# Differential attention: the 32 rotary rows of a head's query and key tiles gathered by DMA, turned together, and put back

## The chip, the cores and the metric

The kernel runs on one core of one Trainium2 chip. The metric is the time of one launch in microseconds (us) of the device, as the median of several runs. TensorE is called PE here, VectorE DVE, ScalarE ACT, GpSimd POOL and SyncE SP, as the profile does.

## The reference, cut to what matters

Two transformer blocks of two layers each on 512 tokens of width 1024, in float32. The second mixer of the first block is differential attention with 8 heads. Each head has two query and two key parts of 64 dimensions, and the first 16 dimensions of every part are rotated:

```python
def _rope(x, positions, theta):          # x: (..., d), d = 16 here
    ang = positions * theta ** (-arange(0, d, 2) / d)
    x1, x2 = x[..., :d // 2], x[..., d // 2:]
    return concatenate([x1 * cos(ang) - x2 * sin(ang), x2 * cos(ang) + x1 * sin(ang)], -1)

q, k, v = split(x @ w_qkv, 3)            # q, k: 16 parts of 64, rope on the first 16 of each
p1, p2 = causal_softmax(q1 @ k1.T / 8), causal_softmax(q2 @ k2.T / 8)
o = (p1 - lam * p2) @ v                  # per head, 128 wide
o = rmsnorm(o, subln) * (1 - lambda_init)
return o.reshape(b, s, 1024) @ w_o
```

## The kernel before

The program is a row of eight phases: latent attention, a feed-forward layer, differential attention (`diff`), a feed-forward layer, then the four layers of the second block. All activations stay on chip; weights stream in by DMA on SP's queue into two buffers (`raw`). Each fp32 matmul is done as three products of a high and a low part (lines 347 to 349: high by high, low by high, high by low). For that every weight tile is cast into `whi` by ACT (line 313) and its rest `wlo` is formed by DVE (line 314), up to five tiles ahead.

In `diff`, q and k of a head are 128x512 tiles (rows: two parts of 64 dimensions; columns: tokens), made in PSUM by 24 matmuls each (`pj`; `ps` for the first two heads). `evac(h, which)` takes a finished tile: `rope` turns it, then `split` and a copy cast it into what the score matmuls read: two casts `qa` and four casts `ka` on ACT (64x512 each), the low part of q on POOL, the low part of k on DVE (`xd`). These lines of `rope` are what the change replaces, 16 tiles in all:

```python
nc.vector.stream_shuffle(t2, src, swap)                   # L653, 128x512, from PSUM
nc.vector.tensor_tensor(t1, src, C, op=ALU.mult)          # L654
nc.vector.tensor_tensor(t2, t2, Sn, op=ALU.mult)          # L655
nc.gpsimd.tensor_tensor(t1, t1, t2, op=ALU.add)           # L656
```

`scores(h, qt)` makes the two score tiles `s` of a block of 128 queries (128 x 128, 256, 384 and 512 columns for qt 0 to 3), DVE takes the row maxima (L589), ACT the exponentials (L592), DVE joins both (`xc`, L1041 to L1043), PE transposes the result (`pt`, L353), ACT and DVE split it (`xa`, `xb`), and `value` multiplies it by V (`o`). `post` takes the norm: ACT squares and copies `o` (L1050, L1052), PE sums (`sps`), POOL takes the power (`rr`, L1067), PE spreads it (`bp`), DVE multiplies (L1074), ACT and POOL split the result into `VH` and `VL`.

Between the score groups the projection of the next head is spread (`fills`, table `n`), and work that follows a result is put off by `defer(delay, f)`: it is issued once the matmuls written since have passed the delay on a clock that counts matmul columns. A scheduler then orders PE, ACT, DVE and SP by its own estimates; POOL keeps the order of the program in `diff`. The first 128x128 scores of head h+1 follow the 128x512 scores of head h.

Of the kernel before, what the change touches and what calls it, by code (L numbers as in the profile page):

```python
# [9 lines left out]
F32 = mybir.dt.float32  # L10
F32R = mybir.dt.float32r
I32 = mybir.dt.int32
AF = mybir.ActivationFunctionType
ALU = mybir.AluOpType
# [3 lines left out]
D = 1024  # L18
S = 512
# [3 lines left out]
LAMBDA_INIT = 0.8 - 0.6 * math.exp(-0.3)  # L23
DFF1, DFF2 = 4096, 2816
MLA_SWAP = [i ^ 16 for i in range(32)]
DIFF_SWAP = [i ^ 8 if i < 16 else i for i in range(32)]
RING = 5
RAW = 2
AUTO = True
# [1 line left out]

PLAN = {
    "mla": dict(hand=("SP", "Pool"), ln=7000, sm=6000, pv=2500, eb=3, gate=5, cq=1500, n=([5] * 4 + [6] * 4) * 3 + [5] * 4 + [9] * 4),
    "diff": dict(hand=("Pool",), qp=1, kp=0, vp=1, wp=0, rp=0, nb=2, ln=7000, rot=3500, sm=6500, pv=2500, eb=3, sums=1000, scale=5500, n=[30] * 4 + [11] * 24 + [9] * 4),
    "fox": dict(ln=5500, sm=4200, pv=1500, eb=2, n=[30] * 4 + [11] * 24 + [9] * 4),
    "ret": dict(ln=5500, y=3900, n=30),
    "f0": dict(ln=7000), "f1": dict(ln=8500), "g0": dict(ln=5500), "g1": dict(ln=5500),
# [3 lines left out]
class Net:  # L41
# [617 lines left out]

    def rope_tables(self, pool, tmp, which, tags=("t0", "t1", "t2"), bufs=1):  # L660
        nc = self.nc
        C = pool.tile([128, S], F32, name="ropeC", bufs=1)
        Sn = pool.tile([128, S], F32, name="ropeS", bufs=1)
        pi = tmp.tile([128, S], I32, tag=tags[0], name="pi", bufs=bufs)
        a = tmp.tile([128, S], F32, tag=tags[1], name="ang", bufs=bufs)
        k = tmp.tile([128, S], F32, tag=tags[2], name="kk", bufs=bufs)
        inv = self.col[:, 2 * which:2 * which + 1]
        sgn = self.col[:, 2 * which + 1:2 * which + 2]
        (nc.gpsimd if which else nc.sync).dma_start(out=pi, in_=self.A["positions"].to_broadcast([128, S]))
        nc.vector.tensor_copy(a, pi)  # L670
        nc.vector.tensor_scalar(a, a, inv, None, op0=ALU.mult)
        MAG = 12582912.0
        nc.vector.tensor_scalar(k, a, 1.0 / (2 * math.pi), MAG, op0=ALU.mult, op1=ALU.add)
        nc.vector.tensor_scalar(k, k, -MAG, None, op0=ALU.add)
        c1 = 6.28125
        c2 = float(np.float32(2 * math.pi - c1).view(np.int32) & -4096)
        c2 = float(np.int32(np.float32(2 * math.pi - c1).view(np.int32) & -4096).view(np.float32))
        c3 = float(np.float32(2 * math.pi - c1 - c2))
        for cc in (c1, c2, c3):
            nc.vector.scalar_tensor_tensor(a, k, -cc, a, op0=ALU.mult, op1=ALU.add)  # L680
        PIF = 3.1415925
        nc.vector.tensor_scalar(a, a, PIF, -PIF, op0=ALU.min, op1=ALU.max)
        nc.scalar.activation(Sn, a, AF.Sin)
        nc.vector.scalar_tensor_tensor(a, a, -1.0, a, op0=ALU.mult, op1=ALU.min)
        nc.vector.tensor_scalar(a, a, math.pi / 2, None, op0=ALU.add)
        nc.scalar.activation(C, a, AF.Sin)
        nc.vector.tensor_scalar(Sn, Sn, sgn, None, op0=ALU.mult)
        return C, Sn

    def setup(self):  # L690
# [268 lines left out]
    def diff(self):  # L959
        nc, A, tc = self.nc, self.A, self.tc  # L960
        mm = nc.tensor.matmul
        with ExitStack() as outer:
# [27 lines left out]
            kls = [kz[:, 2 * i:2 * i + 2, :] for i in range(2)]  # L990
            places = self.whole("c", F32)

            def evac(h, which):
                def f(ps):
                    r = self.rope(p, ps, DIFF_SWAP, C, Sn)


                    if which == 0:
                        qk[h] = [self.rs(n, F32R).rearrange("p (a n) -> p a n", a=2) for n in ("qa", "ka")]
                        qk[h].append(kls[h % 2])  # L1000
                    q, k, kl = qk[h]
                    for i in range(2):
                        own, other = slice(64 * i, 64 * i + 64), slice(64 - 64 * i, 128 - 64 * i)
                        if which == 0:
                            self.split(q[own, i, :], q[other, i, :], r[own], eng=nc.gpsimd if self.plan["qp"] else None)
                        else:
                            self.split(k[own, i, :], kl[own, i, :], r[own], eng=nc.gpsimd if self.plan["kp"] else None)
                            nc.scalar.copy(k[other, i, :], r[own])
                    ready.add((h, which))
                return f  # L1010

            self.fhead(4, lambda i, ps: evac(i // 2, i % 2)(ps))
            for _ in self.v_half(VH, VL, 0):
                pass

# [32 lines left out]
            def post(h, o):  # L1048
                sq = places[:, 3, :]
                nc.scalar.activation(sq, o, AF.Square)  # L1050
                ot = p.tile([128, S], F32, tag="ot", name="ot", bufs=1)
                nc.scalar.copy(ot, o)  # L1052
                rr = self.small(4, "rr")

                def sums():
                    sps = self.ps("sps")
                    for t in range(NT):
                        mm(sps[:, 2 * t:2 * t + 2], sq[:, t * 128:t * 128 + 128], ones, start=(t == 0), stop=(t == NT - 1))
                        self.tick(128, 4)
                    s8 = self.small(8, "s8")  # L1060
                    nc.vector.tensor_copy(s8, sps[:, 0:8])

                    nc.vector.tensor_tensor(rr, s1[h], s1[h], op=ALU.mult)
                    nc.vector.tensor_scalar(rr, rr, 1e-6, None, op0=ALU.mult)
                    nc.vector.scalar_tensor_tensor(rr, s8.rearrange("p (t a) -> p t a", a=2)[:, :, 0], 1.0 / 128, rr,
                                                   op0=ALU.mult, op1=ALU.add)
                    nc.gpsimd.tensor_tensor(rr, rr, self.mh, op=ALU.pow)  # L1067
                    self.defer(self.plan["scale"], scale)

                def scale():  # L1070
                    bp = self.ps("bp")
                    for t in range(NT):
                        self.transpose(bp[:, t * 128:t * 128 + 128], rr[:, t:t + 1].to_broadcast([128, 128]))
                    nc.vector.scalar_tensor_tensor(ot, ot, sub, bp, op0=ALU.mult, op1=ALU.mult)  # L1074
                    self.split(VH[:, h, :], VL[:, h, :], ot, eng=nc.gpsimd if self.plan["vp"] else None)
                    nready[0] = h + 1

                self.defer(self.plan["sums"], sums)
# [334 lines left out]
ROPE_ORDER = np.array([16 * (i // 32) + i % 16 + 32 * (i % 32 // 16) for i in range(64)])  # L1413


def constants():
    c = {}
    c["c_idn"] = np.eye(128, dtype=np.float32)
    i = np.arange(128)
    c["c_mask"] = np.zeros((128, S), np.float32)  # L1420
    c["c_mask"][:, S - 128:] = np.where(i[None, :] <= i[:, None], 0.0, NEG)
    col = np.zeros((128, 16), np.float32)
    col[:, 0] = (10000.0 ** (-2.0 * (ROPE_ORDER[i % 64] % 32) / 64.0)).astype(np.float32)
    col[:, 1] = np.where(ROPE_ORDER[i % 64] < 32, -1.0, 1.0)
    d = i % 64
    col[:, 2] = np.where(d < 16, 500000.0 ** (-2.0 * (d % 8) / 16.0), 0.0).astype(np.float32)
    col[:, 3] = np.where(d < 8, -1.0, np.where(d < 16, 1.0, 0.0))
    c["c_col"] = col
    rows = np.zeros((32, 16), np.float32)
    r = np.arange(32)  # L1430
    kind = r // 8
    rows[:, 0] = kind == 0
    rows[:, 1] = kind == 1
    rows[:, 2] = kind >= 2
    rows[:, 3] = -1.0 * (kind == 2)
    rows[:, 4] = -1.0 * (kind == 3)
    rows[:, 5] = kind < 2
    rows[r, 8 + r % 8] = 1.0
    c["c_rows"] = rows
    inv = (10000.0 ** (-np.arange(128) / 128.0)).astype(np.float32)  # L1440
    ang = (np.arange(S, dtype=np.float32)[None, :] * inv[:, None]).astype(np.float32).astype(np.float64)
    c["c_rcos"] = np.cos(ang).astype(np.float32)
    c["c_rsin"] = np.sin(ang).astype(np.float32)
    key, q = np.arange(128)[:, None], np.arange(S)[None, :]
    dec = np.zeros((4, 128, S), np.float32)
    for h in range(4):
        gam = 1.0 - 2.0 ** (-5.0 - h)
        dec[h] = np.where(q // 64 >= key // 64, gam ** np.abs(q - key), 0.0)
    c["c_decay"] = dec
    return c  # L1450


def layout(I):
    A = dict(constants())
# [36 lines left out]
        A[f"w_in{i}"] = gu.reshape(n // 2, 4, 128, D)[1:]  # L1491
        A[f"w_out{i}"] = pack_h(np.asarray(I["ffn_w_out_2"])[i])

    def heads(w):
        q, k = pack_f(w[:, :D]), pack_f(w[:, D:2 * D])
        v = np.concatenate([pack_v(np.ascontiguousarray(w[:, 2 * D + j * 512:2 * D + j * 512 + 512])) for j in range(2)])
        qk = np.stack([q, k], axis=1).reshape(16, 128, D)
        return np.concatenate([qk[:4], v, qk[4:]])

    A["w_d"] = heads(np.asarray(I["diff_w_qkv"])[0])  # L1500
    A["w_do"] = pack_h(np.asarray(I["diff_w_o"])[0])
    wx = np.asarray(I["fox_w_in_2"])[0]
    A["w_x"] = heads(wx[:, :3 * D])
# [29 lines left out]
```

## Time and profile before

| | us |
|---|---|
| median of 3 runs | 2502.1 (2501.55 to 2502.84) |
| profiled execution, its own time | 2498.99 |
| span in the profile | 2497.1 |
| PE busy | 2443.6 (98%) |
| DVE busy | 1655.0 (66%) |
| ACT busy | 1114.1 (45%) |
| POOL busy | 347.9 (14%) |

The span runs from the first to the last instruction; the execution's own time holds 1.9 us more around it. Busy time is time in which an instruction runs on the engine. PE is busy nearly throughout, so the end of the kernel moves by what PE's idle stretches gain or lose. `diff` lies at about 545 to 800 us of the span.

### The profile page before, as it was taken

What the parts mean: (1) busy time and instruction counts of PE and PEld (TensorE: products, weight loads), DVE (VectorE), ACT (ScalarE), POOL (GpSimd) and SP (SyncE); (2) the same over time, 40 slices, a digit from 0 to 9 for tenths busy, and PEclk for the clock granted to TensorE, in tenths of its full rate; (3) what the DMA queues carried; (4) which work ended last, traced back from release to release, by engine and by line L of the source; (5) the groups of instructions that cost most, each with busy time, mean ns of one, the idle gap of its engine ahead of it and who ended that gap; (6) DMA issues with size and microseconds to landing.
All of it is one profiled execution on the core that took longest, in us unless ns stands there. A gap on an engine that the chain in (4) does not pass through costs nothing.

```text
span 2497.1 us, 35898 instructions
## 1 busy us (share of the span) xinstructions
PE 2443.6 (98%) x14612; PEld 2173.6 (87%) x14612; DVE 1655.0 (66%) x2294; ACT 1114.1 (45%) x1664; POOL 347.9 (14%) x311
## 2 busy tenths in 40 slices
PE   8999999999989999999999999999999999999998
PEld 7889889887778988987888999988888888999987
DVE  6978758656987956755655877744455455777743
ACT  5634535424663543544454544543322233444532
POOL 2103012012342201103000222100000000222100
PEclk9999999999999999999999999999999999999999
DMA  4323232323121333232312233232422223233232
GB/s 151 109 68 116 92 107 88 102 79 93 60 85 51 119 99 106 83 110 77 94 59 85 90 114 102 85 102 77 129 82 82 87 85 101 85 121 108 77 102 76
DMA packets 65861, 233.41 MB, mean 93 GB/s; under 512 B 7536, under 2 KB 7680, under 8 KB 65696
## 3 DMA queue, kind: packets, MB, share of 16 engines
q1 hardware_dynamic: 62064, 219.21, 27.4%
q0 software_dynamic: 3488, 11.55, 1.5%
q8 instruction: 114, 1.87, 0.3%
q14 instruction: 51, 0.42, 0.1%
q10 hardware_dynamic: 144, 0.36, 0.0%
HBM read 228.99 MB, written 2.10 MB: 93 GB/s over the span
## 4 chain that ended last, share of the span: by engine, by line
PE 52%; DVE 1%; issue 0%; ACT 0%; POOL 0%; DMA 0%; DVEq 0%; POOLq 0%; ACTq 0%
PE zA L266 3%; PE zA L267 3%; PE zA L268 3%; PE ta L348 2%; PE ta L349 2%; PE ta L347 2%; PE tb L348 2%; PE tb L347 2%; PE tb L349 2%; PE ps L347 2%; PE ps L348 2%; PE ps L349 2%; PE pj L347 2%; PE pj L349 2%; PE pj L348 2%; PE v L347 2%
## 5 line engine op out<-in xcount | busy, mean ns | idle before, releaser
L314 DVE TENSOR_TENSOR wlo<-raw,whi 128x1024 fp32r<-128x1024 f32 (+3 forms) x347 | 432.8, 1249 | 294.2 <-ACT whi L313 293.8
L313 ACT CAST whi<-raw 128x1024 fp32r<-128x1024 f32 (+3 forms) x347 | 359.5, 1038 | 579.4 <-PE ta L349 129.1
L314 DVE TENSOR_TENSOR wlo<-qt,whi 128x1024 fp32r<-128x1024 f32 x102 | 164.2, 1610 | 36.8 <-ACT whi L313 36.8
L347 PE MATMUL ps<-XH,whi 128*128 128x256 f32 (+1 forms) x576 | 178.6, 310 | 2.3 <-ACT XH L313 2.3
L348 PE MATMUL ps<-XL,whi 128*128 128x256 f32 (+1 forms) x576 | 177.5, 308 | 0.1
L349 PE MATMUL ps<-XH,wlo 128*128 128x256 f32 (+1 forms) x576 | 177.1, 308 | 0.0
L267 PE MATMUL zB<-XL,whi 128*128 128x256 f32 x544 | 154.0, 283 | 0.4 <-DVE XL L314 0.4
L266 PE MATMUL zB<-XH,whi 128*128 128x256 f32 x544 | 154.0, 283 | 0.0
L268 PE MATMUL zB<-XH,wlo 128*128 128x256 f32 x544 | 153.9, 283 | 0.0
L313 ACT CAST whi<-qt 128x1024 fp32r<-128x1024 f32 x102 | 107.1, 1050 | 91.8 <-PE zA L267 59.6
L196 POOL TENSOR_TENSOR qt<-qr,raw 128x1024 f32<-128x1024 f32 x34 | 87.1, 2560 | 367.6 <-PE ta L348 204.2
L349 PE MATMUL ta<-whi,jt 128*128 128x512 f32 x320 | 124.1, 390 | 3.0 <-DVE jt L314 3.0
L196 POOL TENSOR_TENSOR qt<-raw,qt 128x1024 f32<-128x1024 f32 x34 | 87.7, 2579 | 272.6 <-DVE wlo L314 248.1
L347 PE MATMUL ta<-whi,jt 128*128 128x512 f32 x320 | 124.8, 390 | 0.0
L348 PE MATMUL ta<-wlo,jt 128*128 128x512 f32 x320 | 124.6, 389 | 0.0
L347 PEld LDWEIGHTS ps<-XH,whi 128*128 128x128 f32 x576 | 110.5, 192 | 7.5 <-ACT XH L313 2.6
L347 PE MATMUL pj<-XH,whi 128*128 128x512 f32 x288 | 116.7, 405 | 0.0
L348 PEld LDWEIGHTS ps<-XL,whi 128*128 128x128 f32 x576 | 110.6, 192 | 5.7 <-DVE XL L314 0.8
L349 PEld LDWEIGHTS ps<-XH,wlo 128*128 128x128 f32 x576 | 110.5, 192 | 5.1
L349 PE MATMUL pj<-XH,wlo 128*128 128x512 f32 x288 | 113.0, 392 | 0.0
L348 PE MATMUL pj<-XL,whi 128*128 128x512 f32 x288 | 112.5, 391 | 0.0
L267 PEld LDWEIGHTS zB<-XL,whi 128*128 128x128 f32 x544 | 104.4, 192 | 0.6 <-DVE XL L314 0.6
(469 smaller groups left out, 7378.7 us busy)
## 6 DMA issues: line engine op xcount, KB each, us to landing
raw<-in_w_r SPq DMA_DIRECT2D x48, 512.0 KB, 3.5
raw<-in_w_out SPq DMA_DIRECT2D x44, 512.0 KB, 3.5
qr<-in_w_in SPq DMA_DIRECT2D x40, 512.0 KB, 4.5
raw<-in_w_in SPq DMA_DIRECT2D x40, 512.0 KB, 3.5
raw<-in_w_d SPq DMA_DIRECT2D x24, 512.0 KB, 3.5
raw<-in_w_x SPq DMA_DIRECT2D x24, 512.0 KB, 3.5
raw<-in_w_dn0a SPq DMA_DIRECT2D x16, 512.0 KB, 3.4
raw<-in_w_dn0b SPq DMA_DIRECT2D x16, 512.0 KB, 3.5
```

Source lines behind the costliest of these rows:

```text
L196: eng.tensor_tensor(t, a, b, op=ALU.subtract)
L266: mm(out, a, sh[:, k, :], start=f, stop=False, skip_group_check=True)
L267: mm(out, a, sl[:, k, :], start=False, stop=False, skip_group_check=True)
L268: mm(out, b, sh[:, k, :], start=False, stop=e, skip_group_check=True)
L313: nc.scalar.copy(hi, src)
L314: (eng or nc.vector).tensor_tensor(lo, src, hi.bitcast(F32), op=ALU.subtract)
L347: mm(ps, ah, bh, start=first, stop=False)
L348: mm(ps, ah, bl, start=False, stop=False)
L349: mm(ps, al, bh, start=False, stop=last)
```

## The change

A q or k tile is no longer turned where it is. The columns of the weights are permuted on the host so that the 32 rotary rows of a tile are rows 48 to 79, with each pair side by side. ACT copies the tile from PSUM to `rq`, and three DMAs on ACT's queue bring the rotary rows into `rot` and, with the two rows of each pair exchanged, into `swp`. q and k of a head share the two: `rot` holds 64 rows, `swp` 64 rows at 64 to 127. When the k tile is in, `turn(h)` is deferred by 3000: two multiplications and an addition on 64x512 on DVE, then two DMAs on POOL's queue that put the rows back into the two `rq`. It defers `parts(h)` by 4500: the same casts and low parts as before, now from `rq`. Cosine and sine share one table. The norm weight `sub` is applied in ACT's copy of `o`, and DVE's last step is a plain multiplication.

```diff
@@ PLAN["diff"]
-rot=3500, sm=6500, ...
+rot=3000, back=4500, sm=6500, ...
@@ def diff
             def evac(h, which):
                 def f(ps):
-                    r = self.rope(p, ps, DIFF_SWAP, C, Sn)
+                    if which == 0:
+                        got[h] = [[], p.tile([128, S], F32, tag="rot", name="rot", bufs=1),
+                                  p.tile([128, S], F32, tag="swp", name="swp", bufs=1)]
+                    rs, rot, swp = got[h]
+                    r = p.tile([128, S], F32, tag="rq", name="rq", bufs=2)
+                    rs.append(r)
+                    nc.scalar.copy(r, ps)
+                    o = 32 * which
+                    nc.scalar.dma_start(out=rot[o:o + 32], in_=r[48:80])
+                    nc.scalar.dma_start(out=swp[64 + o:96 + o:2], in_=r[49:80:2])
+                    nc.scalar.dma_start(out=swp[65 + o:96 + o:2], in_=r[48:80:2])
+                    if which == 1:
+                        self.defer(self.plan["rot"], lambda: turn(h))
+                return f
+
+            def turn(h):
+                rs, rot, swp = got[h]
+                a, b = rot[0:64], swp[0:64]
+                nc.vector.tensor_tensor(a, a, C[0:64], op=ALU.mult)
+                nc.vector.tensor_tensor(b, swp[64:128], Sn[64:128], op=ALU.mult)
+                nc.vector.tensor_tensor(a, a, b, op=ALU.add)
+                for w in range(2):
+                    nc.gpsimd.dma_start(out=rs[w][48:80], in_=rot[32 * w:32 * w + 32])
+                self.defer(self.plan["back"], lambda: parts(h))
+
+            def parts(h):
+                for which, r in enumerate(got.pop(h)[0]):
...
                     ready.add((h, which))
-                return f
-
-            self.fhead(4, lambda i, ps: evac(i // 2, i % 2)(ps))
+                for which, ps in enumerate(held):
+                    evac(1, which)(ps)
+                held.clear()
+
+            held = []
+            self.fhead(4, lambda i, ps: held.append(ps) if i > 1 else evac(0, i)(ps))
...
-                nc.scalar.copy(ot, o)
+                nc.scalar.activation(ot, o, AF.Copy, scale=sub)
...
-                    nc.vector.scalar_tensor_tensor(ot, ot, sub, bp, op0=ALU.mult, op1=ALU.mult)
+                    nc.vector.tensor_tensor(ot, ot, bp, op=ALU.mult)
@@ module
+_turn = np.arange(16) // 2 + np.arange(16) % 2 * 8
+DIFF_ORDER = np.concatenate([np.arange(16, 64), _turn, 64 + _turn, np.arange(80, 128)])
```

The order of the instructions moves with it, in `diff` alone. On ACT, between the last scores of one head and the first of the next, the program before has this (`e` and `xc` on L592 are exponentials, `VH` is the norm's result, `qa` the query's casts; the `ka` casts stand further on, ahead of the 128x384 exponentials):

```order
L592 ACTIVATE xc,s_6540<-xc,mx 128x512 [waits DVE_49]
L592 ACTIVATE e_6704,r<-e_6704,mx 128x512 [waits DVE_49]
L313 CAST whi<-raw 128x1024 [waits DMAHW4_49,PE_49]
L313 CAST xa<-pt 128x3x128 [waits PE_49]
L313 CAST VH<-ot 128x512 [waits DVE_49]
L592 ACTIVATE xc,s_6756<-xc,mx 128x128 [waits DVE_49]
L313 CAST qa<-rt_6742 64x512 [waits Pool_49]
L313 CAST qa<-rt_6742 64x512
L592 ACTIVATE e_6767,r<-e_6767,mx 128x128 [waits DVE_49,Activation_49]
```

The changed program has this at the same place (`rq` is the copied tile, `DMASW` the put-back on POOL's queue):

```order
L312 CAST xa<-pt 128x3x128 [waits PE_49]
L591 ACTIVATE e_6733,r<-e_6733,mx 128x512 [waits DVE_49]
L312 CAST whi<-raw 128x1024 [waits DMAHW2_49,PE_49]
L312 CAST VH<-ot 128x512 [waits DVE_49]
L312 CAST qa<-rq 64x512 [waits DMASW6_49]
L312 CAST qa<-rq 64x512
L312 CAST ka<-rq 64x512 [waits DMASW7_49]
L1040 CAST ka<-rq 64x512
L312 CAST ka<-rq 64x512
L1040 CAST ka<-rq 64x512
L1007 COPY rq<-pj 128x512 [waits DMAHW4_49,DMAHW5_49,PE_49,Pool_49]
L591 ACTIVATE xc,s_6780<-xc,mx 128x128 [waits DVE_49]
```

All six casts have moved from the head's own row to the place before its first exponentials. Before, those casts are of the head after the one whose scores stand beside them; now they are of the head whose 128x128 scores come next.

On PE, from the transposes after the 128x512 scores of one head to the first scores of the next, before:

```order
L353 MATMUL pt<-idn,xc 128x128 [waits DVE_49,PE_49]
L353 MATMUL pt<-idn,xc 128x128 x2
L349 MATMUL pj<-XH,wlo 128x512
L353 MATMUL bp<-idn,rr 128x128 [waits Pool_49]
L353 MATMUL bp<-idn,rr 128x128 x3
L1032 MATMUL s<-ka,qa 128x128 [waits Activation_49]
L1032 MATMUL s<-ka,qa 128x128 [waits PE_49,Activation_49]
L1034 MATMUL s<-xd,qa 128x128 x2
```

And in the changed program:

```order
L352 MATMUL bp<-idn,rr 128x128 [waits PE_49,Activation_49,Pool_49]
L352 MATMUL bp<-idn,rr 128x128 x3
L346 MATMUL pj<-XH,whi 128x512
L347 MATMUL pj<-XL,whi 128x512
L348 MATMUL pj<-XH,wlo 128x512
L1067 MATMUL s<-ka,qa 128x128 [waits PE_49,Activation_49,Pool_49]
L1069 MATMUL s<-xd,qa 128x128 [waits DVE_49]
L1067 MATMUL s<-ka,qa 128x128 [waits PE_49,Activation_49,Pool_49]
L1069 MATMUL s<-xd,qa 128x128 [waits DVE_49]
```

The first scores now wait for POOL and DVE too, that is, for the low parts of q and k, and the two parts of the head have come apart.

On DVE, before the 128x512 maxima of a head, the changed program has the three steps of `turn` (L1019 to L1021; L588 are the maxima, `DMAHW` the gathers on ACT's queue). Before, nothing there waits for a DMA:

```order
L1077 SCALAR_TENSOR_TENSOR r<-r,s_6780,few 128x1 [waits DVE_49]
L313 TENSOR_TENSOR xb<-pt,xa 128x2x128 [waits Activation_49]
L1078 SCALAR_TENSOR_TENSOR xc<-e_6891,r,xc 128x384 [waits DVE_49]
L1020 TENSOR_TENSOR swp<-swp,ropeC 64x512 [waits DMAHW4_49,DMAHW5_49,DMAHW1_49,DMAHW0_49]
L588 ISA xc,mx<-s,mask 128x512 [waits PE_49]
L588 ISA mx 128x1
L1021 TENSOR_TENSOR rot<-rot,swp 64x512 [waits DVE_49]
L588 ISA e_6954,mx<-s,mask 128x512 [waits PE_49]
```

The last step of `turn` now stands between the two maxima, so the put-back of a head starts after the 128x512 scores of the head before it.

## Rows read from the trace of the kernel before

**Rows 1.** Waits of PE, 540 to 800 us: total us, times, longest.

```profile
PE pt L353 <- DVE xc L1043: 8.9, 7, 1.6
```

**Rows 2.** Timeline of PE, one head: start us, length us, instruction, [idle before, releaser].

```profile
685.54 0.42 PE L1032 MATMUL s<-ka,qa 128*128 128x128 f32 x2
...
686.01 0.44 PE L347 MATMUL pj<-XH,whi 128*128 128x512 f32 x1
...
692.93 0.50 PE L347 MATMUL o<-xa,VH 128*128 128x512 f32 x1 [0.31 <-ACT xa L313]
693.66 0.50 PE L348 MATMUL o<-xb,VH 128*128 128x512 f32 x1 [0.22 <-DVE xb L314]
...
701.00 0.39 PE L347 MATMUL pj<-XH,whi 128*128 128x512 f32 x1
...
706.15 0.42 PE L1032 MATMUL s<-ka,qa 128*128 128x128 f32 x2
```

**Rows 3.** Timeline of ACT, the same head.

```profile
690.63 1.26 ACT L313 CAST qa<-rt 64x512 fp32r<-64x512 f32 x2 [0.66 <-POOL rt L656]
...
699.19 0.62 ACT L313 CAST ka<-rt 64x512 fp32r<-64x512 f32 x1 [2.34 <-POOL rt L656]
...
701.77 0.62 ACT L592 ACTIVATE xc<-xc,mx 128x384 f32<-128x384 f32 x1
...
703.23 0.72 ACT L592 ACTIVATE xc<-xc,mx 128x512 f32<-128x512 f32 x1
...
704.56 0.72 ACT L592 ACTIVATE e<-e,mx 128x512 f32<-128x512 f32 x1 [0.51 <-DVE mx L589]
...
705.28 1.03 ACT L313 CAST whi<-raw 128x1024 fp32r<-128x1024 f32 x1
706.22 0.47 ACT L313 CAST xa<-pt 128x384 fp32r<-128x384 f32 x1
707.31 0.62 ACT L313 CAST VH<-ot 128x512 fp32r<-128x512 f32 x1 [0.62 <-DVE ot L1074]
```

**Rows 4.** Timeline of DVE, the same head.

```profile
699.85 0.68 DVE L314 TENSOR_TENSOR xd<-rt,ka 64x512 fp32r<-64x512 f32 x1 [1.16 <-ACT ka L313]
...
702.49 0.68 DVE L589 CUSTOM_DVE_ANT_0 xc<-s,mask 128x512 f32<-128x512 f32 x1
```

**Rows 5.** Timeline of POOL, the same head.

```profile
691.33 2.85 POOL L314 TENSOR_TENSOR qa<-rt,qa 64x512 fp32r<-64x512 f32 x2 [0.73 <-ACT qa L313]
```

**Rows 6.** Lines 653 and 655 in 540 to 800 us: ns min/median/max, first and last start, forms.

```profile
L653 DVE STREAM_SHUFFLE rt<-pj x12: 728/738/756, 625.3 to 735.9; 128x512 f32<-128x512 f32 x12
...
L655 DVE TENSOR_TENSOR rt<-rt,ropeS x16: 670/685/1298, 563.5 to 737.5; 128x512 f32<-128x512 f32 x16
```

**Rows 7.** DMA issues: times, KB each, median us from issue to landing.

```profile
raw<-in_w_xf SPq DMA_DIRECT2D x1, 128.0 KB, 1.9
idn<-in_c_idn POOLq DMA_DIRECT2D x1, 64.0 KB, 4.4
...
lam<-in_diff_lambda_k POOLq DMA_DIRECT2D x2, 32.0 KB, 6.0
...
few<-in_c_rows POOLq DMA_DIRECT2D x1, 2.0 KB, 2.9
```

**Rows 8.** Timeline of ACT and PE: start of the phase; an earlier wait.

```profile
593.13 1.04 ACT L313 CAST whi<-raw 128x1024 fp32r<-128x1024 f32 x1 [3.91 <-DMA raw<-in_w_d]
...
596.09 0.50 PE L347 MATMUL v<-whi,XH 128*128 128x512 f32 x1 [3.15 <-DVE VL L314]
...
254.19 0.38 PE L266 MATMUL zA<-xb,whi 128*128 128x256 f32 x1 [3.23 <-ACT ntmp L286]
```

**Rows 9.** Windows of 10 us: busy time of each engine, PEclk (share of the full clock), DMA.

```profile
250.00:260.00 10.00, 6.77 (x57) 6.56 (x55) 7.27 (x7) 6.40 (x9) 2.88 (x2) 1.00 0.25 85
590.00:600.00 10.00, 6.85 (x26) 5.22 (x26) 6.39 (x14) 4.82 (x10) 0.00 (x0) 0.87 0.47 157
600.00:610.00 10.00, 10.00 (x46) 8.40 (x46) 4.30 (x11) 3.51 (x7) 0.00 (x0) 0.95 0.35 107
```

More of the change, by code (lines that the diff above doesn't have):

```diff
@@ L25 @@
 MLA_SWAP = [i ^ 16 for i in range(32)]
-DIFF_SWAP = [i ^ 8 if i < 16 else i for i in range(32)]
 RING = 5
@@ L33 @@
     "mla": dict(hand=("SP", "Pool"), ln=7000, sm=6000, pv=2500, eb=3, gate=5, cq=1500, n=([5] * 4 + [6] * 4) * 3 + [5] * 4 + [9] * 4),
-    "diff": dict(hand=("Pool",), qp=1, kp=0, vp=1, wp=0, rp=0, nb=2, ln=7000, rot=3500, sm=6500, pv=2500, eb=3, sums=1000, scale=5500, n=[30] * 4 + [11] * 24 + [9] * 4),
+    "diff": dict(hand=("Pool",), qp=1, kp=0, vp=1, wp=0, rp=0, nb=2, ln=7000, rot=3000, back=4500, sm=6500, pv=2500, eb=3, sums=1000, scale=5500, n=[30] * 4 + [11] * 24 + [9] * 4),
     "fox": dict(ln=5500, sm=4200, pv=1500, eb=2, n=[30] * 4 + [11] * 24 + [9] * 4),
@@ L661, in rope_tables @@
         nc = self.nc
-        C = pool.tile([128, S], F32, name="ropeC", bufs=1)
-        Sn = pool.tile([128, S], F32, name="ropeS", bufs=1)
+        C = Sn = pool.tile([128, S], F32, name="ropeC", bufs=1)
+        if not which:
+            Sn = pool.tile([128, S], F32, name="ropeS", bufs=1)
+        lo, hi = (slice(64, 128), slice(0, 64)) if which else (slice(0, 128),) * 2
         pi = tmp.tile([128, S], I32, tag=tags[0], name="pi", bufs=bufs)
@@ L682, in rope_tables @@
         nc.vector.tensor_scalar(a, a, PIF, -PIF, op0=ALU.min, op1=ALU.max)
-        nc.scalar.activation(Sn, a, AF.Sin)
+        nc.scalar.activation(Sn[lo], a[lo], AF.Sin)
         nc.vector.scalar_tensor_tensor(a, a, -1.0, a, op0=ALU.mult, op1=ALU.min)
         nc.vector.tensor_scalar(a, a, math.pi / 2, None, op0=ALU.add)
-        nc.scalar.activation(C, a, AF.Sin)
-        nc.vector.tensor_scalar(Sn, Sn, sgn, None, op0=ALU.mult)
+        nc.scalar.activation(C[hi], a[hi], AF.Sin)
+        nc.vector.tensor_scalar(Sn[lo], Sn[lo], sgn[lo], None, op0=ALU.mult)
         return C, Sn
@@ L991, in diff @@
             places = self.whole("c", F32)
+            got = {}
             def evac(h, which):
                 def f(ps):
-                    r = self.rope(p, ps, DIFF_SWAP, C, Sn)
+                    if which == 0:
[23 more added lines that the diff above has]
+                for which, r in enumerate(got.pop(h)[0]):
                     if which == 0:
@@ L1424, in constants @@
     col[:, 1] = np.where(ROPE_ORDER[i % 64] < 32, -1.0, 1.0)
-    d = i % 64
-    col[:, 2] = np.where(d < 16, 500000.0 ** (-2.0 * (d % 8) / 16.0), 0.0).astype(np.float32)
-    col[:, 3] = np.where(d < 8, -1.0, np.where(d < 16, 1.0, 0.0))
+    col[:, 2] = (500000.0 ** (-2.0 * (i % 16 // 2) / 16.0)).astype(np.float32)
+    col[:, 3] = np.where(i % 2, 1.0, -1.0)
     c["c_col"] = col
@@ L1492, in layout, with heads @@
         A[f"w_out{i}"] = pack_h(np.asarray(I["ffn_w_out_2"])[i])
-    def heads(w):
+    def heads(w, order=None):
+        if order is not None:
+            w = w[:, np.concatenate([np.tile(order, 16) + 128 * (np.arange(2048) // 128), np.arange(2 * D, 3 * D)])]
         q, k = pack_f(w[:, :D]), pack_f(w[:, D:2 * D])
@@ L1498, in heads @@
         return np.concatenate([qk[:4], v, qk[4:]])
-    A["w_d"] = heads(np.asarray(I["diff_w_qkv"])[0])
+    A["w_d"] = heads(np.asarray(I["diff_w_qkv"])[0], DIFF_ORDER)
     A["w_do"] = pack_h(np.asarray(I["diff_w_o"])[0])
```

## The prediction

> **What bounds the kernel now.** PE is busy for 2443.6 of 2497.1 us, so I look only at where PE stands still, and first at its waits inside the phase. The largest is the transposes `pt` waiting for DVE's `xc`: 8.9 us in 7 times, once per head [rows 1]. Then I read one head from its first scores to those of the next head. They start at 685.54 and 706.15: a period of 20.61 us [rows 2]. In it stand the `pt` wait (1.6 at the longest, which I use [rows 1]) and 0.31 and 0.22 ahead of `o` [rows 2], together 2.1. Without them PE alone would need 18.5. The head's last scores end at 701.00, where the next projection begins; 15.0 us pass from the end of its first scores (686.01) to there, 14.46 without the two `o` waits [rows 2]. The same head on ACT shows where its casts stand: the two `qa` at 690.63, the four `ka` from 699.19 to 701.77, all of them done more than 4 us ahead of the scores at 706.15 that are the first ones of another head [rows 3]. So ACT's casts are hidden now. Last I look at the start of the phase: PE waits 3.15 us at 596.09, because ACT waited 3.91 us for a weight at 593.13 with the casts of V behind it [rows 8].
>
> **What the edits cost where they are hidden.** DVE drops per tile a shuffle of 0.74 and two operations of about 0.68 [rows 6], 4.2 us per head, and gains three operations on 64 rows; an operation on 64 rows takes 0.68 as well [rows 4], so 2.0. DVE gains 2.2 us of room per head, and the `pt` wait, which ends with DVE's `xc`, is what this room could pay back: at most 1.6 per head. POOL drops two additions per head; ACT gains two copies and six DMA issues. Spread over 20 us they fit, since ACT stands still for 0.5 to 2.3 us several times in the head [rows 3]. The norm weight moves into an ACT copy that is there anyway; I take nothing for it. The program order of the phases before and after stays as it is, so nothing else enters the sum.
>
> **What is moved: the casts.** In the new order all six casts stand on ACT between the last exponentials of one head and the first of the next, and PE's next instruction behind its projections are the scores that need them. The turn ends between the two maxima of the last scores, so the casts can't come much earlier than they stand. I add up ACT from the end of the last scores, each step at its distance in this head [rows 3, 4]:
> - DVE's maximum, to the start of ACT's first exponential: 0.74 (702.49 to 703.23).
> - The exponential with its sum: 0.82. `xa`: 0.47. The second exponential: 0.72 (704.56 to 705.28). `whi`: 0.94 (705.28 to 706.22). `VH`: 0.62.
> - Two `qa`: 1.26, with the gap behind them 1.29. Four `ka`: 2.58 (699.19 to 701.77).
>
> That is 8.18 us. POOL's low part of q starts with the first `qa` and needs 2.85 for both [rows 5]: it is done at 4.31 + 0.62 + 2.85 = 7.8, just inside. The second score pair adds 0.24. After that PE runs its 14.46 to the end of the head's last scores. New period: 8.18 + 0.24 + 14.46 = 22.88 against 20.61, **2.27 us more per head**. What PE has to do meanwhile, twelve projection matmuls, three transposes and `bp`, took 706.15 - 701.00 - 1.6 = 3.6 us in this head [rows 1, 2], so some 5 us remain open; the `pt` and `o` waits of before vanish behind them. Before, the cover of these casts was PE's projections in mid-head; this cover is gone.
>
> **The put-back.** The trace before has no transfer from SBUF to SBUF, so I bound its landing by other rows. Below: 1.9 us for 128 KB on SP's queue. Above: 6.0 for 32 KB on POOL's queue. Between: 2.9 for 2 KB and 4.4 for 64 KB on POOL's queue [rows 7]. I take 3.0, near the lowest of POOL's rows, because those at 4.4 and 6.0 were issued in a bunch with others and these are two. The turn's last step ends 1.4 after the scores (maximum 0.69, then 0.68 [rows 4]); the casts reach `qa` at 4.31, so 2.9 is hidden and 0.1 shows. At 4.4 it is 1.5 per head, at 6.0 3.1; at 1.9 nothing. The Trainium skill (DMA: Bandwidth & Descriptors, Anatomy of one DMA — SWDGE (gpsimd) path) gives about 2.0 us fixed plus bytes over 436e3 for such a queue; an estimate from that page is 2.15 us for 64 KB, and by it the put-back would be hidden wholly and the sum would be 1 us lower. The row of 2.9 for 2 KB is longer than the rule. Of the gathers on ACT's queue the k tile's are the late ones; by the 1.9 us of the row on a hardware queue, well ahead of the 128x512 maxima, I take nothing for them, and 1.5 per head at most, if they land as late as 4.4 and hold up the maxima behind them on DVE.
>
> **Clock.** PE's wait of 3.15 us is followed by a stretch in which the granted clock falls to its lower level: the window's mean is 0.87, the next one's 0.95 [rows 8, 9]. That is (0.13 + 0.05) x 10 = 1.8 us of work lost. Another wait of 3.23 us at 254.19 shows no such fall (1.00) [rows 8, 9]. The new waits are one of some 4 to 5 us per head, longer than either. I take one fall for each of the three heads with the full wait, 3 x 1.8 = 5.4; both ends, 0 and 5 x 1.8 = 9, are kept.
>
> **The sum**, by heads:
> - Start: the weight wait stays, but V's casts now stand elsewhere to it; of PE's 3.15 I take 2.0 off (0 to 3.5): -2.0.
> - Into head 2, where `VH` doesn't stand before the casts: 2.27 - 0.62, and the put-back 0.7 less covered: +2.4.
> - Into head 3 the casts come ahead of the last exponential, so that 0.72, 0.47 and 0.62 fall out of the chain: +0.4.
> - Into heads 4, 5 and 6 the steady case: 3 x (2.27 + 0.1) = +7.1.
> - Into head 7 the output projection fills in: between 0 and 2.3, I take +1.0.
> - Clock: +5.4.
>
> Together +14.3. On the profiled execution, 2498.99, this is 2513.3; the median of the runs is 3.1 above it, so **2502.1 + 14.3 = 2516 us**.
>
> **Rivals.**
> 1. *No fall of the clock*: the same chain without 5.4: 2511. For it speaks the wait at 254.19, against it the one at 596.09.
> 2. *The put-back lands late.* POOL issues and handles its transfers while DVE works through the turn and the softmax; the row with 6.0 is of a time with several issues in a row [rows 7]. At 6.0 heads 2 and 4 to 6 each pay 3.0 more, head 3 about 2: +14 with the falls, 2530; with 4.4 about 2522. The Trainium skill (SBUF — State Buffer, the box on DMA issued by GpSimd in "SBUF: two separate sides") says that such a transfer waits while DVE holds the port pair that both share, and that ACT's or SP's queue is free of this; no row here separates the two, and by it this rival would be the likelier one.
> 3. *Faster: DVE was the limit.* If the casts are done by the time PE has run out of projections, 3.6 us after the last scores, each head falls to PE's own 18.5: 6 x 2.1 = 12.6 less, with the start's 2.0 and its fall of 1.8 also gone: 2486. It decides at 3.6 against my 8.2: ACT would have to run the casts before the exponentials of the last scores, as into head 3, and the turn would have to be done by then. For it: `pt` is PE's one regular wait and it ends with DVE. Against it: the new order puts the turn's end behind the first maximum.
> 4. *They cancel*: the start gains its 3.5 and 1.8, the clock doesn't fall, and heads 2 and 7 cost 1 less each: 2502.1 + 8.9 - 1.5 - 1.8 - 2 = 2506, within 0.2% of before.
>
> **Chances and range.** My case 0.38, no fall 0.20, late landing 0.17, cancel 0.13, faster 0.12. A measurement of this kernel tells about 0.2%, 5.0 us, from no change: faster means below 2497.1, slower above 2507.1. So slower 0.75, same 0.13, faster 0.12. The range leaves out the faster rival and a landing beyond 6 us: 2500 to 2536. The likeliest case alone spans 2511 to 2522, by the landing and the clock.
>
> **What would show it.** After the change, PE's list of waits in the phase has the scores `s` waiting for ACT (`ka`) or POOL (`qa`) some 5 us per head, and `pt` no longer waits for DVE. The period of heads 4 to 6 is 22.9 us, and with a fall of the clock up to 24.7. ACT's `qa` shows no or little idle time before it; if it shows 1 us or more with the put-back as releaser, the landing is late. DVE's busy time falls by some 8 x 2.2 = 17 us. I am wrong if `s` waits under 3 us per head or if the period is below 20.6.

## The result, and the profile after

The changed kernel takes 2525.0 us (median of 4 runs, 2523.5 to 2528.1) beside 2501.8 us for the kernel before: a ratio of 1.0095, 95% interval 1.0083 to 1.0107. It is 23 us slower. The forecast was 2516 with a range of 2500 to 2536. A trace holds one execution: that of before is 3.1 us faster than the median of its runs, that of the changed kernel 1.5 us, so the traces differ by a little more than the medians.

The page of the changed kernel begins with the span and the busy times:

```profile
span 2521.7 us, 36008 instructions
PE 2458.0 (97%) x14612; PEld 2185.4 (87%) x14612; DVE 1641.2 (65%) x2254; ACT 1122.5 (45%) x1680; POOL 329.7 (13%) x311
```

The same 14612 matmuls keep PE busy 14.4 us longer (2458.0 against 2443.6). The span grew by 24.6, so PE stands still only 10.2 us more. DVE has 13.8 us less to do and is not rewarded for it. Two losses are to be found: waits, and matmuls that got slower.

PE's waits in 540 to 830 us (total, times, longest):

```profile
PE s L1067 <- POOL qa L313: 14.7, 6, 4.6
PE s L1067 <- ACT ka L1040: 8.1, 3, 7.5
PE sps L1093 <- ACT xc L1085: 2.8, 4, 1.2
...
PE pt L352 <- DVE xc L1078: 0.6, 2, 0.4
```

The regular wait of before [rows 1] has shrunk from 8.9 to 0.6 us. In its place the first scores of a head wait for the casts, 22.8 us in all. The rows of three of these heads, from PE's timeline (the longest is the wait into head 2):

```profile
644.51 0.44 PE L1067 MATMUL s<-ka,qa 128*128 128x128 f32 x1 [7.51 <-ACT ka L1040]
...
693.08 0.45 PE L1067 MATMUL s<-ka,qa 128*128 128x128 f32 x1 [4.62 <-POOL qa L313]
...
720.14 0.30 PE L1067 MATMUL s<-ka,qa 128*128 128x128 f32 x1 [3.91 <-POOL qa L313]
...
721.44 0.47 PE L1067 MATMUL s<-ka,qa 128*128 128x128 f32 x1 [0.81 <-POOL qa L313]
...
724.08 0.63 PE L347 MATMUL pj<-XL,whi 128*128 128x512 f32 x1
724.51 0.63 PE L348 MATMUL pj<-XH,wlo 128*128 128x512 f32 x1
...
728.89 0.39 PE L347 MATMUL pj<-XL,whi 128*128 128x512 f32 x1
729.11 0.39 PE L348 MATMUL pj<-XH,wlo 128*128 128x512 f32 x1
```

From 693.08 to 720.14 the period is 27.1 us, against 20.61 before [rows 2]. The last four rows show the second loss. Behind the wait a projection matmul starts every 0.43 us; from 728.9 on, every 0.22. The windows (third to seventh column busy times, then PEclk) say the same:

```profile
590.00:600.00 10.00, 9.62 (x46) 7.87 (x45) 6.48 (x13) 8.20 (x18) 3.01 (x2) 1.00 0.29 88
...
690.00:700.00 10.00, 6.20 (x15) 4.82 (x16) 5.30 (x13) 5.71 (x13) 5.33 (x4) 0.52 0.36 120
...
720.00:730.00 10.00, 8.98 (x30) 7.30 (x31) 3.71 (x14) 4.08 (x12) 3.51 (x3) 0.66 0.32 113
```

A mean of 0.52 and 0.66 says that the granted clock is at its lower level, 1.2 GHz, for nearly all of the first of these two windows and for two thirds of the second. At the start of the phase the wait and the fall of before [rows 8, 9] are gone: 9.62 and 1.00.

ACT in the same head, from the last exponentials on, with POOL's and DVE's last steps:

```profile
713.25 0.73 ACT L591 ACTIVATE xc<-xc,mx 128x512 f32<-128x512 f32 x1 [3.39 <-DVE mx L588]
...
714.44 0.48 ACT L312 CAST xa<-pt 128x384 fp32r<-128x384 f32 x1 [0.37 <-PE pt L352]
714.81 0.72 ACT L591 ACTIVATE e<-e,mx 128x512 f32<-128x512 f32 x1
...
716.03 1.04 ACT L312 CAST whi<-raw 128x1024 fp32r<-128x1024 f32 x1 [0.41 <-PE pj L347]
716.98 0.61 ACT L312 CAST VH<-ot 128x512 fp32r<-128x512 f32 x1
717.50 1.25 ACT L312 CAST qa<-rq 64x512 fp32r<-64x512 f32 x2
718.78 0.62 ACT L312 CAST ka<-rq 64x512 fp32r<-64x512 f32 x1
...
720.71 0.62 ACT L1040 CAST ka<-rq 64x512 fp32r<-64x512 f32 x1
```

```profile
718.26 3.13 POOL L313 TENSOR_TENSOR qa<-rq,qa 64x512 fp32r<-64x512 f32 x2 [2.78 <-ACT qa L312]
```

```profile
720.71 1.22 DVE L313 TENSOR_TENSOR xd<-rq,ka 64x512 fp32r<-64x512 f32 x1 [0.46 <-ACT ka L312]
```

This is the chain that was forecast [rows 3 to 5], and `qa` starts without a wait for its DMA. The landings, from the page's DMA issues:

```profile
rot<-rq ACTq DMA_DIRECT2D x16, 64.0 KB, 1.9
swp<-rq ACTq DMA_DIRECT2D x32, 32.0 KB, 2.9
rq<-rot POOLq DMA_DIRECT2D x16, 64.0 KB, 1.9
```

In heads 0 and 1 ACT waits for the put-back while PE has other work. From the first scores on, it waits for it only into head 2; the second of the two put-backs there landed after 3.8 us, the longest of all:

```profile
640.52 1.26 ACT L312 CAST qa<-rq 64x512 fp32r<-64x512 f32 x2 [1.81 <-DMA rq<-rot]
643.11 0.62 ACT L312 CAST ka<-rq 64x512 fp32r<-64x512 f32 x1 [1.33 <-DMA rq<-rot]
```

### The profile page after: what moved, and what is told of

It is laid out like the page before. It is cut to its first block, busy times and chain, and to the rows that moved or that the text cites. A ratio compares the mean times of both kernels' runs of the same rounds, so it can differ in the third digit from the quotient of the medians.

```text
span 2521.7 us, 36008 instructions
## 1 busy us (share of the span) xinstructions
PE 2458.0 (97%) x14612; PEld 2185.4 (87%) x14612; DVE 1641.2 (65%) x2254; ACT 1122.5 (45%) x1680; POOL 329.7 (13%) x311
## 4 chain that ended last, share of the span: by engine, by line
PE 49%; DVE 2%; issue 1%; ACT 1%; POOL 1%; DMA 0%; DVEq 0%; POOLq 0%; ACTq 0%
PE zA L265 3%; PE zA L267 3%; PE zA L266 3%; PE ta L346 2%; PE ta L348 2%; PE ta L347 2%; PE tb L348 2%; PE tb L346 2%; PE tb L347 2%; PE ps L347 2%; PE ps L346 2%; PE ps L348 2%; PE pj L346 2%; PE pj L348 2%; PE pj L347 2%; PE v L346 2%
## 5 line engine op out<-in xcount | busy, mean ns | idle before, releaser
L313 DVE TENSOR_TENSOR wlo<-raw,whi 128x1024 fp32r<-128x1024 f32 (+3 forms) x347 | 426.1, 1230 | 294.0 <-ACT whi L312 293.4
L313 DVE TENSOR_TENSOR wlo<-qt,whi 128x1024 fp32r<-128x1024 f32 x102 | 170.4, 1671 | 29.9 <-ACT whi L312 29.8
```

The costliest lines, as they stand in the source:

```text
L313: (eng or nc.vector).tensor_tensor(lo, src, hi.bitcast(F32), op=ALU.subtract)
```

## The experiments

All runs, with the medians of the kernel beside its own kernel before. The phase starts at slightly different times from run to run, so the fourth column gives what the heads themselves take: from the first scores of head 3 to those of head 7, read from PE's timeline, each of one execution. They can differ by some 2 us between kernels of the same time: e5_norm shows 85.9 beside the 83.8 of before, with a fall of the clock (0.66 in 680 to 690 us) that the traced execution of before doesn't have.

| run | us | ratio (95% interval) | heads 3 to 7 |
|---|---|---|---|
| before | 2501.8 | | 83.8 |
| changed | 2525.0 | 1.0095 (1.0083 to 1.0107) | 104.3 |
| g4_no_link | 2503.4 | 1.0008 (0.9999 to 1.0018) | 80.0 |
| e3_no_turn | 2488.7 | 0.9944 (0.9928 to 0.9961) | 74.6 |
| e4_fill | 2523.6 | 1.0086 (1.0071 to 1.0101) | 95.9 |
| e1_early | 2528.9 | 1.0108 (1.0093 to 1.0123) | 102.2 |
| e2_before_early | 2513.2 | 1.0042 (1.0027 to 1.0057) | 86.2 |
| e7_gather_pool | 2523.6 | 1.0094 (1.0079 to 1.0109) | 100.5 |
| e8_pool_14x1 | 2508.1 | 1.0031 (1.0018 to 1.0044) | 87.2 |
| e9_pool_14x2 | 2506.2 | 1.0020 (1.0010 to 1.0030) | 84.1 |
| g3_pool_14x2_qdve | 2503.0 | 1.0006 (0.9996 to 1.0015) | 84.4 |
| g1_q_low_dve | 2528.0 | 1.0110 (1.0095 to 1.0125) | 103.9 |
| e6_sp_back | 2526.2 | 1.0099 (1.0082 to 1.0115) | 104.0 |
| e5_norm | 2502.3 | 1.0006 (0.9997 to 1.0016) | 85.9 |

The theory: the cost is that the casts come after the round trip, behind the last exponentials, so that PE waits for ACT's row and then runs at the lower clock. The main rival: the added work itself costs (issues, transfers, copies, steps of DVE beside POOL).

**g4_no_link: all the work, without the dependency.**

```diff
-nc.gpsimd.dma_start(out=rs[w][48:80], in_=rot[32 * w:32 * w + 32])
+nc.gpsimd.dma_start(out=swp[32 * w:32 * w + 32], in_=rot[32 * w:32 * w + 32])
```

> The changed kernel with the turned rows put back into rows 0 to 63 of swp and not into rq: all copies, gathers, DVE steps and put-backs run, but the casts don't wait for them (q and k go unturned into the scores). PE's order is that of the change; the casts now stand ahead of the last exponentials on ACT. Theory 'the cost is that the casts come after the round trip, behind the last exponentials': no wait of the first scores, no falls behind it, 2492 us (2486 to 2500). Rival 'the added work itself costs (issues on ACT, transfers, DVE beside POOL)': 2510 us or more.

Measured: 2503.4 us. PE's waits in the phase:

```profile
PE s L1067 <- POOL qa L313: 9.9, 8, 5.8
PE pt L352 <- DVE xc L1078: 2.5, 5, 0.8
```

The 5.8 is the wait into head 2, which stays; from head 3 to head 7 the longest wait of the scores is 0.9, the windows of 670 to 770 us show a clock of 1.00, and the four heads take 80.0 us against 104.3. With every instruction still there and one dependency gone, ACT's order moves with it, and 24 us of the heads come back. This decides for the theory. But 2492 was expected and the total is only level with before: the wait into head 2 and its fall remain, and so do the short waits above. The cut isn't complete, either. POOL keeps the order of the program, so q's low part still stands behind the put-backs, whose issue waits for DVE's turn. Rows of one head, ACT's cast and then POOL:

```profile
695.20 1.25 ACT L312 CAST qa<-rq 64x512 fp32r<-64x512 f32 x2
...
705.27 1.08 POOL L1023 DMA_DIRECT2D swp<-rot  x2 [2.40 <-DVE rot L1021]
706.42 2.63 POOL L313 TENSOR_TENSOR qa<-rq,qa 64x512 fp32r<-64x512 f32 x2
```

The casts are done at 696.5 and the low part, for which PE's first scores wait, starts 10 us later. So the `s` waits left here are a rest of the dependency and no clean price of the added work; no run frees them.

**e3_no_turn: copies and casts, without gathers, turn and put-back** (the rotation is left out).

```diff
-nc.scalar.dma_start(out=rot[o:o + 32], in_=r[48:80])
-nc.scalar.dma_start(out=swp[64 + o:96 + o:2], in_=r[49:80:2])
-nc.scalar.dma_start(out=swp[65 + o:96 + o:2], in_=r[48:80:2])
...
-nc.vector.tensor_tensor(a, a, C[0:64], op=ALU.mult)
...
-    nc.gpsimd.dma_start(out=rs[w][48:80], in_=rot[32 * w:32 * w + 32])
```

> The changed kernel without the three gathers, the turn and the put-backs: the rotation is left out, so q and k go unturned; copy, deferral and casts stay. Theory 'place of the casts': without the round trip the casts stand in mid-head again, the first scores don't wait: 2488 us (2482 to 2496). Rival 'the copies on ACT and the held tiles cost': 2510 us or more.

Measured: 2488.7 us, as expected. The waits of PE in the phase are these at the head of the list:

```profile
PE sps L1081 <- ACT xc L1073: 3.3, 5, 0.8
PE o L346 <- ACT xa L312: 1.4, 2, 0.7
```

No wait for the casts, 18.7 us per head: PE's own time is 18.5, as worked out from [rows 2]. This is what a rope that cost nothing would bring, 13.9 us. The copies are harmless. Each taken against its own kernel before, this run and g4_no_link are 16.2 us apart. This is what gathers, turn and put-back cost with the link through POOL still there: 9.5 us of it lie in the two periods that end with the first scores of heads 2 and 3 (23.9 and 24.6 us against 17.7 and 21.3), where g4_no_link has its wait of 5.8 and the fall behind it.

**e4_fill: PE kept at work through the wait.**

```diff
 ss = [self.ps("s") for _ in range(2)]
+if qt == 0 and 2 <= h <= 6:
+    for j in range(20):
+        mm(ss[0], self.XH[:, 0, 0:128], self.XH[:, j % 8, :], start=True, stop=True)
```

> The changed kernel with 20 matmuls of 512 columns into the score tile ahead of the first scores of heads 2 to 6, overwritten by those; they fill 4.5 us of each wait. Theory 'the clock falls because PE waits': the falls behind the waits go, the chain of casts stays: 2510 us (2505 to 2515), period of heads 4 to 6 some 23 us. Rival 'the clock falls for another reason', or the added matmuls delay the scores: 2525 us or more.

Measured: 2523.6 us, a miss in the total. Where the fill fits the wait, it did what was expected; two rows of PE's timeline and a window:

```profile
701.68 0.33 PE L1070 MATMUL s<-ka,qa 128*128 128x128 f32 x1 [0.63 <-POOL qa L313]
...
726.00 0.33 PE L1070 MATMUL s<-ka,qa 128*128 128x128 f32 x1 [0.63 <-POOL qa L313]
```

```profile
690.00:700.00 10.00, 10.00 (x49) 8.26 (x48) 7.44 (x16) 5.75 (x12) 3.25 (x4) 1.00 0.10 20
```

The clock stays at 1.00 and the period is 24.3 us in place of 27.1. So the fall costs 2.8 us in a head of that kind, and the chain without it is 24.3, not the 22.9 of the forecast. The total doesn't follow since the 4.5 us of fill stand ahead of head 3 too, where the changed kernel waited 1.0 us only, and the wait into head 2 is longer than the fill: 3.2 us of it are left, and the clock falls behind them (0.75 in 650 to 660).

**e1_early and e2_before_early: the projections spread earlier.** The same two edits, on the changed kernel and on the one before.

```diff
-n=[30] * 4 + [11] * 24 + [9] * 4
+n=[30] * 4 + [14] * 4 + [11] * 20 + [9] * 4
...
-while self.unit < 4 * h - 4 - (i == 0):
+while self.unit < 4 * h - 4 - (i == 0) - 1:
```

> The changed kernel with the q and k projections of heads 2 to 7 spread earlier by about one score group (table n: 14 instead of 11 in head 1's four places, gate one unit earlier); the DMAs, DVE's turn and the casts themselves are as in the change, but all six casts now stand on ACT ahead of the 128x384 exponentials of the head before. Theory 'place of the casts': the wait of the first scores (4 to 8 us per head) and the falls of the clock behind it go, and with DVE relieved the head comes near PE's own 18.5 us: 2488 us (2482 to 2496). Rival 'the round trip through DMA and the extra ACT work cost in themselves': 2510 us or more.

> The kernel before with the same earlier projections and nothing else. Theory: its casts were hidden already, and the wait of the transposes for DVE stays at 1.5 us per head: 2500 us (2496 to 2504). Rival 'the earlier projections are a gain in themselves': the same as the run beside it, about 2488 us.

Both missed: 2528.9 and 2513.2. The gate's line stands a second time in the later phase `fox`, where it is edited too; from its first matmul `z` to its last `tb` that phase takes 204.9 us in the traces with the edit and without, so the difference lies in `diff`. The earlier projections are a loss in themselves, 10.5 us on the kernel before, so e1 is no clean test of the casts' place. They did stand early and the scores' long wait was gone, but another took its place, one of 3.43 us in each of three heads. PE's first wait in the list, and ACT in one head (`ACTq` are the issues):

```profile
PE o L346 <- ACT xa L312: 14.5, 5, 3.4
```

```profile
704.02 0.51 ACT L591 ACTIVATE xc<-xc,mx 128x256 f32<-128x256 f32 x1
704.15 0.51 ACTq L1009 DMA_DIRECT2D rot<-rq  x1
...
704.70 0.61 ACTq L1010 DMA_DIRECT2D swp<-rq  x1
705.34 0.61 ACTq L1011 DMA_DIRECT2D swp<-rq  x1
706.00 0.51 ACT L591 ACTIVATE e<-e,mx 128x256 f32<-128x256 f32 x1 [1.38 <-DVE wlo L313]
```

The projections no longer stand ahead of the value product `o`, and ACT's `xa` for it comes behind three issues of 0.5 to 0.6 us, which hold the next exponential. That one starts as the third issue ends; DVE's `wlo`, which the profile names as its releaser, had ended at 705.09.

**e7_gather_pool, e8_pool_14x1, e9_pool_14x2: gathers on POOL's queue, and then a smaller shift of the projections.**

```diff
-nc.scalar.dma_start(out=rot[o:o + 32], in_=r[48:80])
+nc.gpsimd.dma_start(out=rot[o:o + 32], in_=r[48:80])
...
-n=[30] * 4 + [11] * 24 + [9] * 4
+n=[30] * 4 + [14] * 1 + [11] * 23 + [9] * 4     (e8; [14] * 2 + [11] * 22 in e9; the gate as in e1)
```

> The changed kernel with its 48 gathers issued on POOL's queue in place of ACT's; nothing else is edited. In the new order ACT has the casts ahead of the weight's cast and of VH. Theory 'the wait is ACT's row up to the last cast': the row is shorter by those two and by the wait of the weight's cast, about 2 us per head, the wait falls from 4.7 to some 2.5 us and the clock falls less often: 2510 us (2503 to 2516). Rival 'only the casts' being late against the put-back counts, ACT's row doesn't': 2525 us.

> As the run with gathers on POOL's queue, with one place of table n at 14 in place of 11 and the gate one unit earlier: PE has 18 projection matmuls between the last scores and the first of the next head (4.5 us with bp) in place of 12. Theory 'place of the casts': the wait falls by another 1 us per head: 2503 us (2497 to 2510). Rival 'what PE has in between makes no difference': as the run beside it.

> As the run with gathers on POOL's queue, with two places of n at 14 and the gate one unit earlier: in heads 3 and 4 and 6 and 7 the casts now stand ahead of the last exponentials. Theory 'place of the casts': no wait of the first scores there, PE comes near 18.7 us a head, with a wait of about 1 us for xa ahead of the value product, since few projections stand in front of it: 2493 us (2486 to 2500). Rival, after the run with the earliest projections: the waits move to the value product and the clock still falls: 2510 us or more.

Measured: 2523.6, 2508.1 and 2506.2. The first is a miss: the waits of the scores add up to much the same, in other pieces.

```profile
PE s L1067 <- POOL qa L313: 15.3, 7, 4.5
PE s L1069 <- DVE xd L313: 5.8, 6, 1.4
```

ACT's row did get shorter, but POOL's and DVE's low parts now end the chain, the clock still falls, and the heads gain only 3.8 us. With 18 projection matmuls in front of the first scores (e8) the four heads take 87.2 us; the scores' longest wait there is 1.6. With the casts ahead of the last exponentials in part of the heads (e9) they take 84.1, close to the 83.8 of before. Each step that gave the casts more cover took time back, as the theory says; e8 came out within its expectation, e9 13 us above. Part of this is the tail of the phase: from head 7's first scores to the last transposes `tp` e9 takes 67.1 us, before 62.6, with a clock of 0.84 in 770 to 790. Why is not shown: g3 below has the same projections and the same longest waits in its tail (1.8), and in its traced execution the tail takes 63.8 at a clock of 1.00.

**g1_q_low_dve and g3_pool_14x2_qdve: the low part of q on DVE**, on the changed kernel and on e9.

```diff
-qp=1
+qp=0
```

> The changed kernel with the low part of q on DVE in place of POOL. Theory 'POOL and DVE slow each other at the end of the chain' (DVE's low part of k took 1.2 us beside POOL's of q, 0.68 before): the chain ends 0.8 to 1 us earlier per head, 2520 us (2515 to 2523). Rival 'ACT's casts alone end the chain': 2524 us.

> The run with gathers on POOL's queue and two places of n at 14, with the low part of q on DVE as well. Theory: as there, the scores' wait for DVE's low part of k (2.5 us in all) shrinks: 2503 us (2497 to 2507), about the kernel before. Rival 'DVE is the limit again': 2507 us or more.

Measured: 2528.0, a miss, and 2503.0, as expected. On the changed kernel the wait just changes its name:

```profile
PE s L1067 <- DVE qa L313: 13.8, 4, 5.1
PE s L1067 <- ACT ka L1040: 9.4, 4, 7.7
PE s L1069 <- DVE xd L313: 3.6, 4, 1.0
```

In g3, the best complete version that was tried, heads 3 to 7 take 84.4 us (in the fastest of its ten executions) and the ratio to before is 1.0006, its interval holding 1. Nothing here that keeps the rotation beats the kernel before.

**e6_sp_back: the put-backs on SP's queue.**

```diff
-nc.gpsimd.dma_start(out=rs[w][48:80], in_=rot[32 * w:32 * w + 32])
+nc.sync.dma_start(out=rs[w][48:80], in_=rot[32 * w:32 * w + 32])
```

> The changed kernel with the put-backs on SP's queue in place of POOL's. Theory: in heads 3 to 6 they have landed when ACT reaches the casts, so nothing changes there; head 2 alone waited for them: 2524 us (2520 to 2528). Rival after the Trainium skill (SBUF — State Buffer, the box on DMA issued by GpSimd): they are held up by DVE, and another queue gains 1 us or more per head: 2517 us or less.

Measured: 2526.2 us, no gain. The landing on SP's queue:

```profile
DMA to landing us min/median/max: 1.9/1.9/4.2
```

On POOL's it was 1.8/1.9/3.8. Into head 2, where one of POOL's was the late one, SP's both landed after 1.9 us and PE waited 6.1 us in place of 7.5; one execution of each doesn't tell whether the queue did that. What the Trainium skill (SBUF — State Buffer, the box on DMA issued by GpSimd in "SBUF: two separate sides") says of DVE holding up such issues is not seen in heads 3 to 7. The box speaks of DVE operations in a 2-port mode, and no run here shows whether DVE's are such.

**e5_norm: the norm weight alone**, on the kernel before.

```diff
-nc.scalar.copy(ot, o)
+nc.scalar.activation(ot, o, AF.Copy, scale=sub)
...
-nc.vector.scalar_tensor_tensor(ot, ot, sub, bp, op0=ALU.mult, op1=ALU.mult)
+nc.vector.tensor_tensor(ot, ot, bp, op=ALU.mult)
```

> The kernel before with the norm weight applied in ACT's copy and a plain multiplication on DVE, nothing else. Theory: 0.07 us per head on DVE at the most, no change: 2501.5 us, ratio within 0.2%. Rival 'the scaled copy is longer on ACT and shows': up to 1 us more.

Measured: 2502.3 us, no change that can be told, as expected.

## Why the prediction was right, point by point

**Direction and cause: right.** The casts stand on ACT where the order put them, PE's first scores wait for them, and the old `pt` wait goes. g4_no_link shows that this is the cause. The range held by luck: 2525 lies above the 2511 to 2522 of the likeliest case, in the room that was left for a late landing, and what filled it was mostly the clock.

**The chain: right in its members, 1.1 us short.** "Two `qa`: 1.26 ... Four `ka`: 2.58" and the steps ahead of them measured as forecast, but `xa` waited 0.37 for PE, `whi` 0.41, and DVE's last low part of k took 1.22 us beside POOL's of q, where 0.68 stood in [rows 4]. From DVE's first maximum (712.52) to the second pair's last scores (721.99) it is 9.5 us, not 8.4. e4_fill confirms it: a period of 24.3 without falls, not 22.9.

**The clock: the term of the sum that was mis-sized.** "I take one fall for each of the three heads with the full wait, 3 x 1.8 = 5.4." PE's busy time, for the same matmuls, grew by 14.4. A fall costs 2.8 us in such a head and not 1.8 (e4_fill). By twice the share that is missing in the windows' clock, the lower level lasts 9.6 us in 690 to 700 and 6.8 in 720 to 730, against 3.6 at the start of the phase before [rows 9], from which the price was taken. And there are two more falls: behind the wait of 7.5 us into head 2, and one at 660 us.

**The waits: near in the total, by errors that cancel.** PE's idle time grew by 10.2, against 8.9 in the sum. By periods it grew by 6.0 into head 2 (2.4 forecast) and by 10.0 into heads 4, 5 and 6 (7.1); it changed by -2.8 at the start (-2.0), by nothing into head 3 (+0.4), by -0.4 into head 7 (+1.0), and by -2.7 outside the heads, where the sum had nothing.

**The put-back: taken too dear.** 3.0 us were assumed, 1.9 measured, so the 0.1 per head is nothing. The estimate of 2.15 us from the Trainium skill (DMA: Bandwidth & Descriptors, "Anatomy of one DMA — SWDGE (gpsimd) path") was nearer than 3.0; the lower bound, 1.9 on SP's queue [rows 7], was exact. Into head 2 it showed nonetheless. There the turn was late: DVE's second step waited 0.62 us for the gathers at 636.08, for which the sum had nothing, and the last step ended 4.3 us after the start of the first maximum, against 1.3 in the head of 712.52. The second put-back landed after 3.8 us. The step took 6.0 us more (from 19.5 to 25.6 between the first scores of heads 1 and 2) against +2.4.

**Start: better than forecast**, 4.4 us (35.5 to 31.1 between the first scores of heads 0 and 1) against 2.0: the wait of 3.15 and its fall went, all but 0.4 us.

**The heads.** The periods that end with the first scores of heads 3, 4, 5, 6 and 7 are longer than before by 4.2, 3.5, 6.4, 6.4 and 4.1 us. The sum had 0.4 for the first, 2.4 for each of the next three, 1.0 for the last, and the clock's 5.4. A fall behind one head's first scores counts in the next period; so the first of these carries those of head 2.

**The rivals.** The faster one would have needed the casts done within 3.6 us of the last scores; without the dependency the heads do run below their time of before, by 3.8 us over four heads. That fits DVE's relief (`pt` waits 2.5 us in place of 8.9), but one execution of each is a thin base for so little, and at 20.0 us per head it is far from PE's own 18.5. The late landing did not occur in heads 3 to 7, and once into head 2. That the clock doesn't fall is refuted by the windows. DVE's busy time fell by 13.8, where 17 was forecast.

What stays open is how much of the 16.2 us between e3_no_turn and g4_no_link is ACT's issues, how much the turn on DVE, and how much the link through POOL; no run here parts them without moving the order too. Nor does any run vary the two delays, 3000 and 4500, alone.

## What to carry to other kernels

When work on a relieved engine is replaced by a round trip through other engines and queues, count not what each takes but where the last consumer ends up: here the transfers took 1.9 us and in most heads cost nothing, while the six casts behind them moved from a place where PE had work to one where it had none. A wait on PE is to be priced with the stretch at the lower clock behind it, which here cost more than the waits did (14.4 us of busy time against 10.2 of idle). Before giving up on such a change, cut the dependency and keep the work: that run says whether the place or the work is to blame, once it is clear that no engine's order keeps the link, as POOL's did here.

## What was not expected of the hardware

DMA issues on ACT's queue hold ACT. In the changed kernel ACT shows three issues between two exponentials:

```profile
695.48 0.52 ACTq L1009 DMA_DIRECT2D rot<-rq  x1
...
696.09 0.55 ACTq L1010 DMA_DIRECT2D swp<-rq  x1
696.67 0.61 ACTq L1011 DMA_DIRECT2D swp<-rq  x1
697.33 0.40 ACT L591 ACTIVATE e<-e,mx 128x128 f32<-128x128 f32 x1 [1.44 <-issue]
```

The exponential starts when the third is out, 1.44 us after ACT's last work, and the profile finds nothing that it waited for. The issues don't count as busy, so ACT's 45% hides some 3.4 us per head. And a transfer of 64 KB from SBUF to SBUF lands after 1.9 us (median) on each of the three queues that were tried, ACT's, SP's and POOL's.
